# Seven half-width products in place of eight for the up projection of the last two token groups, with sums of weights made in the first group, and stores placed a step behind their data

## The chip, the cores and the metric

The kernel runs on one core of one Trainium2 chip. The metric is the device time of one execution in microseconds, the median of several runs. On the core, TensorE (PE in the profile, with its weight loads as PEld) multiplies, VectorE (DVE), ScalarE (ACT) and GpSimd (POOL) do the elementwise work, and SyncE (SP) issues every DMA of this kernel, from one queue that is worked off in order.

## What is computed

One inference step of a decoder layer with two kinds of mixer, for a prompt of 2048 tokens and 8 single-token samples (2056 columns in all). The model width is 1024, the feed-forward width 4096.

```python
h = rmsnorm(x, ln_mix)
proj = h @ w_in                           # 1024 -> 3592
od = gated_delta(conv(proj[...]), ...)    # 4 heads x 128, chunked over the prompt
oa = dilated_attention(proj[...])         # 8 heads x 64, three (window, dilation) branches
x = x + concat([od, oa]) @ w_out          # 1024 -> 1024
h = rmsnorm(x, ln_ffn)
x = x + square(relu(h @ w_ffn_up)) @ w_ffn_down     # 1024 -> 4096 -> 1024
y = rmsnorm(x, ln_final)
```

The outputs are y for prompt and samples, the new convolution and delta states, and the keys and values (the samples' caches are copied through).

## The kernel before

Tokens lie on the free axis, features on the partitions. The 2056 columns are cut into four groups, `GROUPS`: three of 512 columns and a last one of 520, worked as two pieces of 260. Each group goes through the input projection (`in_proj`, 28 units of 128 output features), the output projection (`out_proj`, 8 units), the up projection (`up`, 32 units) and the down projection (`down`, 8 chunks c of 8 outputs m).

Every dense product is made in three passes at fp32 accuracy: a weight block arrives by DMA as `wraw` (128x1024, 512 KB), ACT rounds it to `whi`, POOL subtracts to get `wlo` in four pieces of 256 columns (`load_w`), and PE adds up whi·hi, whi·lo and wlo·hi (`dense`, line 251) over eight 128-row blocks k, 24 matmuls for one unit and piece; `down` has 12, over four blocks. So POOL's part of a unit is needed for the last third of its matmuls. The split activations `hi`, `lo` stand in a pool of 32 tiles.

Two streams run beside each other. The dense stream goes through the phases in the order in_proj of groups 0 to 3, out_proj and the feed-forward part of groups 0 to 3. The mixer stream (`all_mixers`: delta rule, attention, then the samples, twice over the halves of the prompt) is a chain of Python generators; one step of it is taken after every 10 dense products of 512 columns (`advance`). Where a later phase needs the mixers' result, `drain` takes all steps that are left at once: `drain(1)` before `out_proj(0)`, `drain(3)` before `out_proj(2)`. Counted from the program, the mixers have 558 steps; `drain(1)` takes 15 of them, `drain(3)` takes 5. From group 2 on the dense stream is alone on PE.

`ffn` runs the up units four ahead of `down`: up 0 to 7, down(0), up 8 to 11, down(1), and so on; in chunk 7 the next group's `out_proj` stands ahead of down(7). `norm2` splits the next group's activations while `out_proj` runs. Work that ends later than its phase (`later`, one step after each dense unit) and the evacuations go to the lane "feed", and a scheduler orders the instructions of each engine from the lanes' priorities and its own estimate of when each is ready. Each DMA is issued where the code places it: a store such as `d_dn<-ct` in `evac_c` (line 406) follows its data at once, and everything behind it on SP waits until the data are there.

## Time and profile before

| what | value |
|---|---|
| median of 3 runs | 3067.29 us (3055.7 to 3068.8) |
| the profiled execution's own time | 3051.3 us, with a span of 3049.6 us |
| PE busy / DVE / ACT / POOL | 2922.2 / 1682.6 / 1248.5 / 1380.4 us |
| granted TensorE clock, mean | 0.981 |

The profiled execution is 16 us under the median, so sums are made against 3051.3 us and then carried over to the median. Stretches of time in the profile are given in us from the span's start. By the first evacuations of each phase (lines 1477, 1534 and 1555), out_proj(0) starts near 999, up of group 0 near 1062, down near 1113, out_proj(1) near 1540, out_proj(2) near 2175, the up of group 2 near 2251, out_proj(3) near 2590, and the up of group 3 near 2677. A busy PE is not PE at its peak, since the ends of matmuls are modelled; how fast it streams is read from the distance between evacuations.

### The profile page before, as it was taken

To read this page: it belongs to the slowest core of one execution; us is meant where nothing else is said; L and a number is where in the kernel's file an instruction comes from. 1 tells how busy PE (TensorE), PEld (TensorE's weight loads), DVE (VectorE), ACT (ScalarE), POOL (GpSimd) and SP (SyncE) were. 2 spreads that over 40 slices of the span, in tenths; PEclk is the share of its full clock that TensorE was granted. 3 is DMA by queue.
4 is the path that set the end of the run, shared out by engine and by line. 5 is a ranking of instruction groups with operands and counts; after the bars stand their busy time and mean duration, and the time that the engine had idled before them with its cause. 6 is when DMAs were issued, how large, how long until landed. Compare 5 with 4: busy or idle time off the path is not lost.

```text
span 3049.6 us, 49363 instructions
## 1 busy us (share of the span) xinstructions
PE 2922.2 (96%) x17793; PEld 2453.3 (80%) x17793; DVE 1682.6 (55%) x4200; ACT 1248.5 (41%) x2624; POOL 1380.4 (45%) x1743
## 2 busy tenths in 40 slices
PE   8999998999997999999999999999899999999997
PEld 6778776778896877777877778877788888999997
DVE  7657577665566744444467757467543223443334
ACT  5334335555552444544533433222342333433333
POOL 5546453323331343333344543455455555554554
PEclk9999999999999999999999999999999999999999
DMA  4566866665556555345368467477535444332322
GB/s 154 167 211 219 250 217 162 182 177 143 146 148 196 173 164 147 103 136 140 100 221 252 150 212 214 151 230 248 177 128 190 135 138 162 110 117 92 96 90 77
DMA packets 346643, 497.51 MB, mean 163 GB/s; under 512 B 74776, under 2 KB 245240, under 8 KB 341280
## 3 DMA queue, kind: packets, MB, share of 16 engines
q1 hardware_dynamic: 346400, 494.36, 53.4%
q8 instruction: 141, 2.31, 0.3%
q14 instruction: 102, 0.84, 0.1%
HBM read 413.56 MB, written 147.88 MB: 184 GB/s over the span
## 4 chain that ended last, share of the span: by engine, by line
PE 61%; DVE 4%; DMA 4%; issue 1%; POOL 1%; ACT 1%; SPq 1%; DVEq 0%; POOLq 0%; ACTq 0%
PE dense L251 49%; PE bank L936 2%; PE bank L892 2%; PE bank L949 1%; PE bank L910 1%; POOL wlo L232 1%; DMA dx<-d_dn 1%; PE bank L706 1%; PE bank L708 0%; PE bank L733 0%; PE bank L723 0%; PE bank L742 0%; PE bank L920 0%; DMA dw<-d_gc 0%; DMA dti<-d_t 0%
## 5 line engine op out<-in xcount | busy, mean ns | idle before, releaser
L232 POOL TENSOR_TENSOR wlo<-wraw,whi 128x256 fp32r<-128x256 f32 x1616 | 1269.2, 817 | 1454.0 <-ACT whi L229 868.6
L251 PE MATMUL dense<-s,whi 128*128 128x512 f32 (+2 forms) x8000 | 1689.9, 356 | 27.1 <-ACT whi L229 13.6
L251 PEld LDWEIGHTS dense<-s,whi 128*128 128x128 f32 x8000 | 1301.8, 190 | 237.9 <-issue 19.5
L251 PE MATMUL dense<-s,wlo 128*128 128x512 f32 (+2 forms) x4000 | 887.3, 354 | 0.0
L251 PEld LDWEIGHTS dense<-s,wlo 128*128 128x128 f32 x4000 | 659.6, 190 | 103.8 <-issue 3.7
L229 ACT ACTIVATE whi<-wraw 128x1024 fp32r<-128x1024 f32 x404 | 426.9, 1057 | 699.2 <-PE dense L251 588.3
L1555 DVE TENSOR_TENSOR y<-dense,y 128x512 f32<-128x512 f32 (+1 forms) x320 | 186.4, 583 | 306.1 <-PE dense L251 305.8
L880 ACT ACTIVATE as<-as,as 128x256 f32<-128x256 f32 (+2 forms) x384 | 169.7, 443 | 155.2 <-DVE as L876 153.0
L1534 DVE SCALAR_TENSOR_TENSOR tmp<-dense,rb 128x512 f32<-128x512 f32 (+1 forms) x160 | 93.4, 583 | 231.5 <-PE dense L251 231.0
L876 DVE CUSTOM_DVE_ANT_0 as<-bank,nd 128x256 f32<-128x256 f32 (+2 forms) x384 | 122.1, 350 | 171.3 <-PE bank L936 118.4
L1538 DVE TENSOR_TENSOR s<-tmp,s 128x512 fp32r<-128x512 f32 (+1 forms) x160 | 115.2, 720 | 132.7 <-ACT s L1537 132.6
L1536 ACT ACTIVATE tmp<-tmp 128x512 f32<-128x512 f32 (+1 forms) x160 | 87.6, 548 | 237.0 <-DVE tmp L1534 236.9
L403 DVE SCALAR_TENSOR_TENSOR cy<-cr,cw,cy 128x512 f32<-128x512 f32 (+3 forms) x189 | 148.0, 784 | 29.3 <-ACT cy L401 25.8
L892 PE MATMUL bank<-ident,as 128*128 128x128 f32 (+1 forms) x600 | 110.7, 288 | 3.4 <-ACT as L880 3.1
L892 PEld LDWEIGHTS bank<-ident,as 128*128 128x128 f32 (+1 forms) x600 | 64.1, 137 | 33.2 <-issue 17.4
L936 PE MATMUL bank<-ak,aql 128*128 128x256 f32 x256 | 89.3, 360 | 1.2 <-DVE aql L221 1.1
L1537 ACT ACTIVATE s<-tmp 128x512 fp32r<-128x512 f32 (+1 forms) x160 | 87.4, 547 | 4.5
L936 PE MATMUL bank<-ak,aqh 128*128 128x256 f32 x256 | 88.2, 356 | 0.0
L910 PE MATMUL bank<-ak,aq 128*64 128x64 f32 (+1 forms) x512 | 71.0, 375 | 13.6 <-issue 12.0
L949 PE MATMUL bank<-apt,av 128*64 128x128 f32 x944 | 82.0, 286 | 0.0
L382 ACT ACTIVATE ct<-cy 128x512 f32<-128x512 f32 (+3 forms) x83 | 44.0, 532 | 85.9 <-DVE cy L403 56.1
L383 DVE SCALAR_TENSOR_TENSOR ct<-ct,cy 128x512 f32<-128x512 f32 (+3 forms) x83 | 55.6, 670 | 39.6 <-ACT ct L382 38.8
(345 smaller groups left out, 2667.5 us busy)
## 6 DMA issues: line engine op xcount, KB each, us to landing
wraw<-wdn SPq DMA_DIRECT2D x132, 512.0 KB
wraw<-wup SPq DMA_DIRECT2D x128, 512.0 KB
wraw<-win SPq DMA_DIRECT2D x112, 512.0 KB
s_wk<-ck SPq DMA_DIRECT2D x64, 511.8 KB
s_wv<-cv SPq DMA_DIRECT2D x64, 511.8 KB
d_nak<-nak SPq DMA_DIRECT2D x16, 1024.0 KB
wraw<-wout SPq DMA_DIRECT2D x32, 512.0 KB
nak<-d_nak SPq DMA_DIRECT2D x16, 1024.0 KB
```

Source lines behind the costliest of these rows:

```text
L229: nc.scalar.activation(hi, raw, AF.Copy)
L232: nc.gpsimd.tensor_tensor(out=lo[:, c], in0=raw[:, c], in1=hi[:, c], op=OP.subtract)
L251: self.last = nc.tensor.matmul(p[:, :n], a[:, wo + k * 128:wo + (k + 1) * 128], x[k][:, off:off + n], start=first and i == 0 and k == ks[0 ...
L403: nc.vector.scalar_tensor_tensor(y[:, :np_], r[:, i:i + np_], self.cw[:, j, i:i + 1], y[:, :np_], op0=OP.mult, op1=OP.add)
L876: nc.vector.tensor_tensor_reduce(out=st[:, hh, :nk], in0=b["s"][hh], in1=b["nd"], op0=OP.add, op1=OP.min, scale=-(2.0 ** -(2 * j + hh + 1) ...
L880: nc.scalar.activation(st[:, hh, :nk], st[:, hh, :nk], AF.Exp, bias=so[:, i, hh:hh + 1], scale=-1.0, accum_out=so[:, i, 2 + hh:3 + hh])
L892: nc.tensor.transpose(pT[:m, w * 128:(w + 1) * 128], b["p"][:, hh, kb * 128:kb * 128 + m], self.ident)
L910: nc.tensor.matmul(p[64 * r:64 * r + 64, 256 * hh:256 * hh + nk], qr[hh][:, n:1024:16], ks[hh].bitcast(F32)[:, n:16 * nk:16], start=True, ...
L936: nc.tensor.matmul(p[:, 256 * hh:256 * hh + 256], x[:, q], ks[hh][:, k], start=n == 0, stop=n == 1)
L949: self.nc.tensor.matmul(po[s64, 128 * i:128 * i + 128], v[:, own - (nkb - 1 - kb) * step, s64], b["pt"][:, hh * nkb + kb, :], start=kb == ...
L1538: nc.vector.tensor_tensor(out=ul[:, s], in0=u[:, :n], in1=uh[:, s], op=OP.subtract)
L1555: self.last_v = nc.vector.tensor_tensor(out=y[m][:, s], in0=p[:, :n], in1=y[m][:, s], op=OP.add).ins
```

## The change

Two consecutive up units (2p and 2p+1) are taken as a 2x2 block matrix: rows are the two units, columns the two halves of k (k 0 to 3, k 4 to 7). The group's columns are cut into two halves too (256 each in group 2, 260 in group 3). In groups 2 and 3 the block product is made with seven products of 12 matmuls (Winograd's form of Strassen's scheme) where eight were.

- While group 0's up units go by, `sums_of_weights` makes four sums of each pair's blocks on POOL (4 adds of 128x512) and splits two of them (2 copies on ACT, 2 subtractions of 128x512 on POOL). Six stores of 256 KB for each of the 16 pairs go to `d_ws` (unsplit sums), `d_wh` and `d_wl` (split sums). The buffers of the split sums `wsh`, `wsl` have one copy each, the raw weights of group 0 and 1 four.
- In groups 2 and 3 `up_pair` loads four weight blocks for a pair: `wa` (unit 2p), `ws` (split sums, by two DMAs straight into whi and wlo), `wt` (unsplit sums), `wb` (half of unit 2p+1). POOL splits in pieces of 512 columns. Seven banks are read by one ACT copy and seven DVE adds.
- `norm2_sums` takes `norm2`'s place ahead of groups 2 and 3: for k 4 to 7 two scaled copies, four subtractions and seven splits of half width.
- After group 1 the weight pools are five deep for wraw, whi and wlo alike (before: wraw five, whi and wlo three); the space goes to the split sums of activations (`H2`).
- Stores: the evacuations of `in_proj` put their stores in a list that is issued one evacuation later (`store`, `flush`), with four buffers for `cy`, `ct`, `xs`. In the mixers a `yield` stands ahead of the stores of `dn_first`, `dn_turn` and `attn_combine`, and behind the loads of `attn_combine`; a `yield` after each of the first eight chunks of `delta_first` is taken out. Counted from the program the mixers now have 576 steps; `drain(1)` takes 18, `drain(3)` takes 20.
- `dynamic_dma_scratch_size=512` leaves more SBUF to the pools, and `late` adds two steps of slack in `rms_steps` after group 1.

```diff
+    def load_parts(self, hi, lo):
+        with self.lane("feed"):
+            w = self.wtile("whi", F32R), self.wtile("wlo", F32R)
+            for t, src in zip(w, (hi, lo)):
+                self.nc.sync.dma_start(t.bitcast(F32), src)
+        return w
...
     def evac_c(self, p, j, c0, n):
...
-        nc.sync.dma_start(self.d_dn[j, :, c0:c0 + np_], o[:, :np_])
+        self.store(self.d_dn[j, :, c0:c0 + np_], o[:, :np_])
...
+    def flush(self, keep):
+        while len(self.stores) > keep + 1:
+            for dst, src in self.stores.pop(0):
+                self.nc.sync.dma_start(dst, src)
...
     def dn_first(self, c):
...
+        yield 1
         nc.sync.dma_start(self.d_nak[c], nak)
...
     def delta_first(self, half):
...
                 yield from self.dn_first(c)
-                if c < 8:
-                    yield 1
...
+    def sums_of_weights(self, p, r1, r2):
...
+        s3 = total(a11, a21, OP.subtract)
+        s1 = total(a21, a22, OP.add)
+        s2 = total(s1, a11, OP.subtract)
+        s4 = total(a12, s2, OP.subtract)
+        yield 1
+        hl = parts(s1)
+        nc.sync.dma_start(self.d_ws[p, :, 0:512], s3)
+        nc.sync.dma_start(self.d_ws[p, :, 512:1024], s4)
+        yield 1
+        store(0, hl)
+        yield 1
+        hl = parts(s2)
+        yield 1
+        store(1, hl)
...
+    def norm2_sums(self, g, y):
...
+            sub(t1, a[:, m:n], a[:, 0:m])
+            sub(t2, b[:, m:n], t1)
+            sub(t3, b[:, m:n], a[:, m:n])
+            sub(t4, b[:, 0:m], t2)
+            for i, x in enumerate((a[:, 0:m], b[:, 0:m], b[:, m:n], t4, t1, t2, t3)):
+                s = self.H2.tile([128, GW], F32R, name="s2", tag="s2") if count < 16 else self.stile()
...
+                self.split(h, l, x, nc.vector)
...
+    def up_pair(self, g, p, h2):
...
+        wa = self.load_w(I["wup"][2 * p], 512)
+        ws = self.load_parts(self.d_wh[p], self.d_wl[p])
+        wt = self.load_w(self.d_ws[p], 512)
+        wb = self.load_w(I["wup"][2 * p + 1][:, 512:1024], 512)
...
+                for j, (a, x) in enumerate(((w[0], 0), (w[0], 1), (w[1], 0))):
+                    for k in range(4):
+                        c = 512 * half + 128 * k
+                        self.last = nc.tensor.matmul(bank[:, :m], a[:, c:c + 128], sets[i][k][x],
+                                                     start=j == 0 and k == 0, stop=j == 2 and k == 3).ins
...
+        q = product(wa, 0, 0)
+        with self.lane("feed"):
+            nc.scalar.activation(c11, q, AF.Copy)
+        q = product(ws, 1, 5)
+        add(c22, q, c11)
+        add(c11, product(wa, 1, 1), c11)
+        self.next_later()
+        add(c12, product(ws, 0, 4), c22)
+        q = product(wt, 0, 6)
+        add(c21, q, c22)
+        add(c22, q, c12)
+        add(c12, product(wt, 1, 2), c12)
+        square(u[0])
+        add(c21, product(wb, 0, 3), c21)
+        square(u[1])
```

Three places show how instructions moved. The first is POOL's row at the start of group 0's up units. `wlo` is the split of a weight block, `dw<-dS` the decay of the delta state in the mixers, `wsum` and `wsl` the sums and their split. Before:

```order
L716 TENSOR_TENSOR dw<-dS,egl 128x512 x4
L232 TENSOR_TENSOR wlo<-wraw,whi 128x256 x12
L716 TENSOR_TENSOR dw<-dS,egl 128x512
L232 TENSOR_TENSOR wlo<-wraw,whi 128x256 x8
L716 TENSOR_TENSOR dw<-dS,egl 128x512
L232 TENSOR_TENSOR wlo<-wraw,whi 128x256 x12
```

And now:

```order
L757 TENSOR_TENSOR dw<-dS,egl 128x512 x4
L257 TENSOR_TENSOR wlo<-wraw,whi 128x256 x12
L1553 TENSOR_TENSOR wsum<-wraw 128x512 x2
L757 TENSOR_TENSOR dw<-dS,egl 128x512
L1553 TENSOR_TENSOR wsum<-wsum,wraw 128x512
L231 TENSOR_TENSOR wsl<-wsum,wsh 128x512
L257 TENSOR_TENSOR wlo<-wraw,whi 128x256 x4
L1553 TENSOR_TENSOR wsum<-wraw,wsum 128x512
L231 TENSOR_TENSOR wsl<-wsum,wsh 128x512
L257 TENSOR_TENSOR wlo<-wraw,whi 128x256 x4
```

Between two units' splits there now stand the six POOL instructions of a pair, and the delta state's decay stands among them.

The second is PE's row at the end of the mixers, ahead of `out_proj(2)`. `bank<-ones,savc` sums the values of one sample (four matmuls, eight samples), rows of 8 and 4 matmuls are `down`, rows of 16 and 8 are units of `out_proj`. Before:

```order
L1384 MATMUL bank<-ones,savc 128x1 x4
L251 MATMUL dense<-s,whi 128x512 x4
L251 MATMUL dense<-s,wlo 128x512 x4
L251 MATMUL dense<-s,whi 128x512 x8
L251 MATMUL dense<-s,wlo 128x512 x4
L1384 MATMUL bank<-ones,savc 128x1 x4
L1389 MATMUL bank<-ident,apr 128x8 x4
L1384 MATMUL bank<-ones,savc 128x1 x4
L251 MATMUL dense<-s,whi 128x512 x16
L251 MATMUL dense<-s,wlo 128x512 x8
```

And now:

```order
L276 MATMUL dense<-s,wlo 128x512 x4
L1427 MATMUL bank<-ones,savc 128x1 x4
L276 MATMUL dense<-s,wlo 128x512 x4
L276 MATMUL dense<-s,whi 128x512 x9
L1427 MATMUL bank<-ones,savc 128x1 x4
L276 MATMUL dense<-s,whi 128x512 x7
L276 MATMUL dense<-s,wlo 128x512 x8
L1427 MATMUL bank<-ones,savc 128x1 x4
L276 MATMUL dense<-s,whi 128x512 x16
L1427 MATMUL bank<-ones,savc 128x1 x4
L276 MATMUL dense<-s,wlo 128x512 x8
L1427 MATMUL bank<-ones,savc 128x1 x8
```

The last six samples now stand among the first three units of `out_proj(2)`, where before only the last two stood behind the last `down`.

The third is SP's row in group 2's up units. Before, one load for each unit (`s_wk`, `s_wv` are pieces of the cache copy):

```order
L227 DMA wraw<-wup 128x1024 x2
L1590 DMA s_wk<-ck 368x356
L227 DMA wraw<-wup 128x1024 x2
L1590 DMA s_wv<-cv 368x356
L227 DMA wraw<-wup 128x1024 x3
```

And now:

```order
L244 DMA whi<-d_wh 128x1024
L244 DMA wlo<-d_wl 128x1024
L252 DMA wraw<-wup 128x1024
L252 DMA wraw<-d_ws 128x1024
L1786 DMA s_wk<-ck 368x356
L252 DMA wraw<-wup 128x512
L244 DMA whi<-d_wh 128x1024
L244 DMA wlo<-d_wl 128x1024
```

The two direct loads of a pair's `ws` stand behind the raw loads of the pair after it, and they have to wait until PE lets go of the whi and wlo tile that is five back.

More of the change, by code (lines that the diff above doesn't have):

```diff
@@ L326, in in_proj @@
                     with self.lane("feed"):
+                        self.flush(1)
                         getattr(self, "evac_" + kind)(p, i, c0, n)
+                        self.stores.append([])
+        with self.lane("feed"):
+            self.flush(0)
         if g == 3:
@@ L1441, in load_mix, with load_m @@
                 yield 1
+    def load_m(self, g, k):
+        g0, n = GROUPS[g][0][0], sum(n for _, n in GROUPS[g])
+        m = self.mtile(g) if g == 3 else self.P.tile([128, GW if g else 512], F32, name="m", tag="tmp" if g else "xs", bufs=None if g else 4)
+        self.nc.sync.dma_start(m[:, :n], self.d_mix[k, :, g0:g0 + n])
+        return m
     def mixed_tiles(self):
@@ L1567, in ffn @@
             uu, h2 = {}, self.next_up
[L1568 to L1569 removed]
+            self.ups(g, 0, h2, uu)
             for c in range(8):
[L1571 to L1572 removed]
+                if c < 7:
+                    self.ups(g, 4 * c + 4, h2, uu)
+                if c == 6 and g == 2:
+                    with self.lane("feed"):
+                        self.coming_m = [self.load_m(3, k) for k in range(2)]
                 if c == 7 and g < 3:
@@ L1603, in program @@
         b = Build(nc, tc, ctx, I, O)
-        b.W, b.ahead = ctx.enter_context(b.pool("W", 3)), 3
+        W = ctx.enter_context(b.pool("W", 3))
+        b.pools = {n: [W] * 3 for n in ("wraw", "whi", "wlo")}
         b.H = ctx.enter_context(b.pool("H", 32))
@@ L1623, in program @@
         Ys.insert(0, ctx.enter_context(b.pool("Y3", 8)))
+        sums = ExitStack()
+        b.SW = sums.enter_context(b.pool("S", 1))
+        b.pools["wraw"] = [W] * 3 + [b.SW]
         def late():
-            b.W, b.ahead = ctx.enter_context(b.pool("W3", 3, side="right")), 5
+            sums.close()
+            W3 = ctx.enter_context(b.pool("W3", 1, side="right"))
+            b.pools = {"wraw": [W] * 3 + [W3] * 2, "whi": [W] * 3 + [W3] * 2, "wlo": [W] * 3 + [W3] * 2}
+            b.turns = {}
+            b.late = True
+            b.H2 = ctx.enter_context(b.pool("H2", 16, side="right"))
             b.out = ctx.enter_context(b.pool("out", 1, side="right"))
```

158 lines of the change are left out of this document (127 added, 31 removed).

## The prediction

> **What bounds the kernel now.** I read the page first, then the busy times by stretch, then the waits, and last the instructions in order of time at the few places where PE stands idle.
>
> ```profile
> span 3049.6 us, 49363 instructions
> PE 2922.2 (96%) x17793; PEld 2453.3 (80%) x17793; DVE 1682.6 (55%) x4200; ACT 1248.5 (41%) x2624; POOL 1380.4 (45%) x1743
> PEclk9999999999999999999999999999999999999999
> ```
>
> PE is busy for 96% of the span at a clock that hardly dips, so only two things can move the time: PE's own work, and the 127 us in which it idles. The stretches tell where those are (columns: PE, PEld, DVE, ACT, POOL busy us with counts, granted clock, DMA share, GB/s).
>
> ```profile
> 450.00:470.00 20.00, 7.10 (x34) 5.23 (x33) 18.79 (x36) 5.62 (x11) 11.30 (x12) 0.78 0.78 193
> 900.00:1000.00 100.00, 81.05 (x723) 71.83 (x724) 61.01 (x202) 30.41 (x95) 23.52 (x30) 0.90 0.63 190
> 1062.00:1113.00 51.00, 49.88 (x235) 39.72 (x234) 26.21 (x53) 22.02 (x35) 27.32 (x38) 1.00 0.63 171
> 1113.00:1540.00 427.00, 425.24 (x2598) 327.14 (x2596) 197.89 (x671) 215.06 (x565) 137.63 (x174) 1.00 0.45 125
> 1540.00:1700.00 160.00, 145.15 (x720) 118.63 (x720) 113.24 (x284) 56.19 (x82) 78.11 (x101) 0.98 0.75 235
> 2100.00:2200.00 100.00, 85.86 (x390) 69.58 (x389) 56.95 (x88) 26.79 (x35) 45.52 (x53) 0.93 0.53 174
> 2251.00:2590.00 339.00, 339.00 (x1480) 274.71 (x1480) 109.13 (x157) 115.62 (x145) 195.80 (x246) 1.00 0.48 154
> 2677.00:3000.00 323.00, 323.00 (x2697) 323.00 (x2697) 106.72 (x232) 109.35 (x175) 165.42 (x224) 1.00 0.32 99
> ```
>
> The feed-forward parts of groups 2 and 3 (the last two rows) have no idle time on PE at all: work taken off PE there is time, as long as nothing else fills the gap. In group 0 (the third and fourth row) PE idles 3 us in 478, but there POOL gets new work. The idle time stands at four places: before the first attention (450 to 470, 12.9 us), in the drain before out_proj(0) (900 to 1000, 19.0 us), in the second half's delta rule (1540 to 1700, 14.9 us), and in the drain before out_proj(2) (2100 to 2200, 14.1 us).
>
> **PE's work in groups 2 and 3.** What a matmul costs is read from distances: evacuations at line 1555 stand 12 matmuls apart, and at the very start the kernel has matmuls of 256 columns in a row.
>
> ```profile
> 2400.19 0.69 DVE L1555 TENSOR_TENSOR y<-dense,y 128x512 f32<-128x512 f32 x1 [2.09 <-PE dense L251]
> 2402.97 0.69 DVE L1555 TENSOR_TENSOR y<-dense,y 128x512 f32<-128x512 f32 x1 [2.09 <-PE dense L251]
> 2802.39 0.43 DVE L1555 TENSOR_TENSOR y<-dense,y 128x260 f32<-128x260 f32 x1 [1.01 <-PE dense L251]
> 2803.83 0.43 DVE L1555 TENSOR_TENSOR y<-dense,y 128x260 f32<-128x260 f32 x1 [1.00 <-PE dense L251]
> 19.82 1.11 PE L251 MATMUL dense<-s,wlo 128*128 128x256 f32 x8
> 20.77 2.06 PE L251 MATMUL dense<-s,whi 128*128 128x256 f32 x16
> 22.67 1.11 PE L251 MATMUL dense<-s,wlo 128*128 128x256 f32 x8
> ```
>
> 512 columns: 2.78 / 12 = 0.2317 us. 260 columns: 1.44 / 12 = 0.1200 us. 256 columns: 24 matmuls from 19.82 to 22.67, 2.85 / 24 = 0.1188 us. Group 2 now has 16 pairs x 7 products x 12 = 1344 matmuls of 256 columns for 32 x 24 = 768 of 512: 159.7 for 177.9 us, a gain of 18.2, not the eighth (22.2) that the count of products promises, since halves cost 2.5% more than a whole. Group 3 was in halves already: 1344 for 1536, 192 x 0.1200 = 23.0 us less. Together **-41.2**. The bounds are tight: if 256 columns took as long as 260, -39.6; at half of 512, -45.
>
> Rule against row: the Trainium skill, "TensorE: Matmul & The Clock Gate", section "Back-to-back issue gap", gives for a stream of weight loads and matmuls a sustained 131 ns at 512 columns and 81 ns at 128, the spacing being set by both operations. On a straight line between them 256 columns would take some 98 ns, an estimate from that page, and group 2's change would be 1344 x 0.098 - 768 x 0.131 = +31 us. This trace disagrees: 0.2317 and 0.1188.
>
> **What feeds PE there.** POOL, DVE and ACT are 58%, 32% and 34% busy in group 2, and a pair adds one half block to POOL's four (+25% on up), and small adds on DVE that read seven banks in turn; they are hidden, and I cost them at nothing. The direct loads of `ws` are not hidden so surely. A pair lasts 84 x 0.1188 = 10.0 us; where two pairs follow each other without a `down` between them, the tile for the second pair's `ws` is let go after the first pair's third product (4.3 us) and needed at the second product of the next (11.4 us): 7.1 us for two blocks of 512 KB, behind raw loads on SP. The nearest rows are one such block alone, and the highest rate seen:
>
> ```profile
> 2175.43 4.06 DMA wraw<-wout
> 2190.00:2200.00 10.00, 10.00 (x45) 8.09 (x44) 4.46 (x5) 3.87 (x5) 5.82 (x8) 1.00 0.99 299
> ```
>
> At 299 GB/s two blocks (1.05 MB) need 3.5 us plus the latency; one after the other 8.1 us, 1.0 us late. There are 9 such places in each group (pairs 1, 2, 3, 5, ... 15), so 0 to +18; side by side is nearer, as both are issued together, and I take **+3**. The traffic grows by 2.6 MB for each chunk of 42 us (62 GB/s on 154), below the 299. `norm2_sums` puts 11 DVE instructions of half width for each of four k behind out_proj's last units: 44 x 0.54 (the row below) = 24 us, under units 5 to 7 and down(7), 16.7 + 22.2 us of PE: hidden, bound 0 to +6.
>
> ```profile
> L1538 DVE TENSOR_TENSOR s<-tmp,s 128x260 fp32r<-128x260 f32 x5 | 2.7, 535 | 2.3 <-ACT s L1537 2.3
> ```
>
> **The sums in group 0.** Sixteen pairs x six POOL instructions of 128x512. Of that size POOL has a row of its own:
>
> ```profile
> L1144 POOL TENSOR_TENSOR ao<-ao,ao 128x512 f32<-128x512 f32 x14 | 18.5, 1320 | 25.8 <-DVE ao L1142 25.2
> L232 POOL TENSOR_TENSOR wlo<-wraw,whi 128x256 fp32r<-128x256 f32 x32 | 25.4, 823 | 25.4 <-ACT whi L229 16.7 <-ACT dw L749 8.3 <-issue 0.4
> ```
>
> 96 x 1.32 = 127 us of POOL. After 1113 it fits: twelve pairs need 95 us, with 137.6 makes 233 of 427. In the eight units from 1062 to 1113 it does not: 27.3 + 24 x 1.32 = 59 us in a stretch of 51, so POOL is the bound there by **+8**. The delta state's decay, which stands among the sums in POOL's row, comes late by up to a pair's 7.9 us; PE's delta steps wait for that in part: **+4**. Behind a late `wsl` the stores wait on SP, and raw weights behind those; ACT's second `wsh` of a pair waits for the store of the first. Where splits run 10 us ahead of PE this is covered. Bounds for all of group 0: 0 (all in POOL's gaps) to +30 (each of the 16 pairs 1.9 us late).
>
> Two-input work on POOL also slows DVE. In the trace line 403's instruction takes 0.74 us and, once POOL runs its splits, 1.21:
>
> ```profile
> 463.06 0.74 DVE L403 SCALAR_TENSOR_TENSOR cy<-cr,cw,cy 128x512 f32<-128x512 f32 x1
> 463.90 3.88 POOL L232 TENSOR_TENSOR wlo<-wraw,whi 128x256 fp32r<-128x256 f32 x4 [1.89 <-ACT whi L229]
> 464.02 1.21 DVE L403 SCALAR_TENSOR_TENSOR cy<-cr,cw,cy 128x512 f32<-128x512 f32 x1
> ```
>
> With DVE at 46% busy from 1113 to 1540, I cost that at nothing; were all its 198 us to overlap with POOL's 127 new ones, it would still have a third of the stretch free.
>
> **The stores and the steps.** Before the first attention PE waits 10.4 us for queries and 2.5 for DVE; the loads of the queries (line 977) stand on SP behind stores of line 406 that wait for DVE.
>
> ```profile
> PE bank L910 <- issue: 10.4, 1, 10.4
> PE dense L251 <- DVE cr L389: 2.5, 1, 2.5
> 461.45 0.33 SPq L406 DMA_DIRECT2D d_dn<-ct  x1
> 462.43 1.09 SPq L977 DMA_DIRECT2D aq<-d_q  x2
> 468.67 0.33 SPq L406 DMA_DIRECT2D d_dn<-ct  x1
> 471.02 0.45 SPq L977 DMA_DIRECT2D aq<-d_q  x1
> ```
>
> The changed order keeps these rows' places, but each store now carries the data of the evacuation before, which are there. The loads then go out some 7 us sooner; DVE is 94% busy in this stretch and becomes the next bound. Between 0 and -12.9 I take **-8**. In the second half's delta rule the waits of line 613 (POOL's `nak`) move off SP, and eight more steps spread its loads; of 14.9 us idle I take **-3** (0 to -10).
>
> ```profile
> SPq L613 <- POOL nak L600: 35.1, 9, 6.7
> ```
>
> The eighteen added steps have a price. Drain(1) takes 18 for 15; at 19.0 us of idle time for 15 steps, three more cost **+4** (0 to +10). Drain(3) takes 20 for 5: five more samples of the value loop fall behind the last dense product that pays for steps. In the trace its end looks like this:
>
> ```profile
> 2169.62 0.95 PE L1384 MATMUL bank<-ones,savc 128*128 128x1 f32 x8
> 2173.70 1.05 PE L1384 MATMUL bank<-ones,savc 128*128 128x1 f32 x8 [2.79 <-DVE savc L1378]
> 2180.68 1.65 PE L251 MATMUL dense<-s,whi 128*128 128x512 f32 x3 [5.93 <-ACT whi L229]
> L1373 DVE TENSOR_TENSOR skt<-skt,apT 128x512 f32<-128x512 f32 x16 | 12.5, 815 | 0.0
> L1378 DVE TENSOR_TENSOR savc<-savc,skt 128x512 f32<-128x512 f32 x16 | 11.5, 717 | 0.2
> ```
>
> PE waits for DVE, and then 5.9 us for a weight that was queued behind the samples' last store. A sample is 3 x 0.815 + 2 x 0.717 = 3.9 us of DVE, five more 19.4. The changed PE row puts three units of out_proj (3 x 24 x 0.2317 = 16.7 us) among them, but DVE must also split that projection's inputs and evacuate it, some 8 us; the fourth unit's weight still waits for the end. 19.4 + 8 - 16.7 = 11, less what the first units' earlier weights save: **+7** (0 to +19).
>
> **Sum.** -41.2 + 3 + 8 + 4 - 8 - 3 + 4 + 7 = -26.2. On the profiled execution that is 3025, on the median of 3067.3, 16 us above it, **3041**. I predict for the median.
>
> **Rivals.**
> A, no change: group 0 gives the gain back. Each of 16 pairs is 1.9 us late (+30 for my +12), and nothing comes from the stores (+11): -26.2 + 18 + 11 = +3, 3070. For it: three engines and SP now wait on each other through buffers with one copy. Against: POOL's gaps after 1113, 289 us for 95.
> B, slower: the direct loads set the pace in groups 2 and 3. SP issues them late, behind raw loads that wait for ACT and POOL. The change is slower by 15 us once the 18 tight places lose 44 together, 2.5 us each - that is, 9.6 us for the 7.1; at 4.06 us each, one block's time again, it is 18 x 4.06 - 3 = +70 on the sum: +44, 3111. Against: SP had no such backlog in group 2, and DMA is at half its share.
> C, the change doesn't do what it says: narrow matmuls are set by their weight loads, which double in number in group 2. For it: at 260 columns PEld is busy for all 323.0 us of the last stretch. Against: the 0.1188 at 256 columns has that already in it; group 2 gains nothing only from 0.2317 x 768 / 1344 = 0.1324 on. Then it is -26.2 + 18.2 = -8, 3059. The page's rule above stands on this rival's side.
>
> **Chances.** My forecast (a gain over 0.5%, 15 us, which is about what a measurement of this kernel tells from no change) 0.66, its own range 3003 to 3052: -41.2 - 12.9 - 10 = -64 at best. A 0.18, C 0.03, B 0.13. So faster 0.66, same 0.21, slower 0.13. The range takes in A whole and leaves B out: 3003 to 3070.
>
> **What would show it.** Evacuations of up in groups 2 and 3 1.42 us apart (1.44 in group 3) and no idle PE; up and down of group 2 through chunk 6 in 321 us for 339. In group 0, POOL near full from 1062 on and PE waiting for wlo, but not after the first `down`. The wait for queries near 460 gone. More idle time before out_proj(2). It is wrong if PE waits for whi or wlo at a pair's second product (B), or for wlo all through group 0 (A).

## The result and the profile after

The change makes the kernel slower: 3095.9 us (median of 4 runs, 3088.6 to 3105.1) against 3065.4 (4 runs, 3055.7 to 3068.8), a ratio of 1.0105 with a 95% interval of 1.0078 to 1.0133. The forecast was 3041, in a range of 3003 to 3070. The profiled execution of the changed kernel has a span of 3092.3 us, in the middle of its runs; the profiled one of before (3049.6) is one of the shortest of its own, so the traces stand 42.7 us apart where the medians stand 30.5.

The page of the changed kernel:

```profile
span 3092.3 us, 50899 instructions
PE 2908.9 (94%) x18177; PEld 2469.0 (80%) x18177; DVE 1857.4 (60%) x4432; ACT 1293.4 (42%) x2712; POOL 1547.6 (50%) x1743
PEclk9999999999998899999999999999999999999999
```

PE is busy for 13.4 us less than before, and idles 183 us for 127. The granted clock dips in two neighbouring slices of the page where it did not before. To see where, both spans are cut at the same events: the first evacuation of out_proj(0), the first of out_proj(1), the last of down(6) in group 1, the first of down in group 2, the first of down in group 3, and the end. Busy time by stretch, before (columns as in the prediction):

```profile
0.00:999.10 999.10, 937.22 (x5932) 780.85 (x5933) 659.23 (x1768) 463.03 (x1182) 412.12 (x512) 0.98 0.62 183
999.10:1642.30 643.20, 631.16 (x3802) 495.70 (x3801) 349.93 (x1060) 302.88 (x713) 240.94 (x309) 1.00 0.53 155
1642.30:2169.80 527.50, 500.95 (x2696) 407.66 (x2694) 351.22 (x769) 169.22 (x275) 250.51 (x306) 0.96 0.62 198
2169.80:2300.80 131.00, 122.28 (x542) 99.66 (x543) 63.77 (x97) 54.51 (x73) 78.37 (x94) 0.96 0.52 167
2300.80:2707.80 407.00, 405.50 (x2140) 345.76 (x2139) 139.26 (x228) 144.39 (x195) 226.65 (x290) 1.00 0.44 143
2707.80:3049.60 341.80, 325.13 (x2691) 323.65 (x2689) 119.23 (x281) 114.50 (x187) 171.78 (x234) 0.98 0.28 89
```

And the changed kernel, cut at the same events:

```profile
0.00:1000.90 1000.90, 938.55 (x5933) 785.56 (x5934) 661.63 (x1769) 462.09 (x1182) 410.29 (x512) 0.97 0.63 183
1000.90:1705.90 705.00, 645.40 (x3717) 504.44 (x3716) 352.88 (x991) 312.93 (x735) 360.97 (x402) 0.95 0.58 171
1705.90:2228.80 522.90, 501.44 (x2738) 408.54 (x2736) 360.58 (x812) 177.41 (x288) 252.88 (x319) 0.97 0.67 210
2228.80:2375.20 146.40, 128.33 (x725) 112.00 (x726) 110.03 (x186) 65.34 (x108) 79.56 (x74) 0.92 0.56 185
2375.20:2770.50 395.30, 389.64 (x2537) 354.65 (x2536) 217.43 (x359) 161.99 (x238) 250.51 (x244) 1.00 0.61 198
2770.50:3092.30 321.80, 305.51 (x2535) 303.85 (x2534) 154.82 (x319) 113.66 (x164) 193.41 (x195) 0.98 0.45 144
```

By rows the difference is +1.8, +61.8, -4.6, +15.4, -11.7 and -20.0, together +42.7. Most of the gain that was forecast for PE lies in the last two rows. The second row, group 0, where the sums are formed, takes all of it back and more: PE idles 59.6 us there for 12.0, though POOL is busy for only 361 of 705 us. The first row ends ahead of the sums, and in the other runs below with the same code up to there it is 994 to 1004 us long; so a few us more or less in it mean nothing.

What PE waits for most in that row (releaser, us in total, times, longest):

```profile
PE bank L932 <- ACT as L920: 10.3, 8, 2.8
PE bank L603 <- DMA dx<-d_dn: 8.1, 1, 8.1
PE bank L950 <- DMA ak<-d_kl: 8.1, 2, 5.7
PE bank L950 <- DMA aq<-d_q: 6.3, 1, 6.3
PE bank L706 <- DMA dt<-d_t: 5.8, 1, 5.8
```

It never waits there for `wlo` or `whi`: the dense products always have their weights. PE waits for attention and the delta rule, for exponentials (ACT) and for loads (SP). One such wait, in order of time, first SP's row and then PE's:

```profile
1246.81 0.45 SPq L1002 DMA_DIRECT2D ak<-d_kh  x1
1254.34 0.32 SPq L1572 DMA_DIRECT2D d_ws<-wsum  x1
1258.34 0.32 SPq L1573 DMA_DIRECT2D d_ws<-wsum  x1
1261.13 0.33 SPq L252 DMA_DIRECT2D wraw<-wdn  x1
1261.56 0.38 SPq L1563 DMA_DIRECT2D d_wh<-wsh  x1
1262.39 0.32 SPq L1563 DMA_DIRECT2D d_wl<-wsl  x1
1262.76 0.48 SPq L1003 DMA_DIRECT2D ak<-d_kl  x1
1269.14 1.16 PE L950 MATMUL bank<-ak,aq 128*64 128x128 f32 x8 [5.69 <-DMA ak<-d_kl]
```

The two halves of a key block are loaded 16 us apart, since four stores of sums stand between them in SP's row and each waits for its sum; PE then stands for 5.7 us. Over the whole of group 0's row, ACT and POOL wait for this on account of the sums:

```profile
ACT wsh L230 <- POOL wsum L1553: 58.2, 16, 7.2
ACT wsh L230 <- DMA d_wh<-wsh: 23.4, 8, 6.8
POOL wsum L1553 <- DMA wraw<-wup: 62.4, 15, 6.1
```

So there were at least four candidates: the stores in SP's row, ACT's `wsh` (behind which attention's exponentials wait), POOL's wait for a raw weight ahead of a sum, and POOL's 124 us of new work as such. PE has sixteen stalls of over 1 us in group 0, 55.5 us in all. I followed each back by hand through the rows: eleven (36.7 us) seem to end at a sum in POOL's row, four of them by way of SP, five by way of ACT, two in POOL's own row. That is a reading and not a measurement; the experiments had to say which of these mattered.

### The profile page after: what moved, and what is told of

Its sections match the earlier page's. It is cut to its first block, busy times and chain, and to the rows that moved or that the text cites. A ratio compares the mean times of both kernels' runs of the same rounds, so it can differ in the third digit from the quotient of the medians.

```text
span 3092.3 us, 50899 instructions
## 1 busy us (share of the span) xinstructions
PE 2908.9 (94%) x18177; PEld 2469.0 (80%) x18177; DVE 1857.4 (60%) x4432; ACT 1293.4 (42%) x2712; POOL 1547.6 (50%) x1743
## 5 line engine op out<-in xcount | busy, mean ns | idle before, releaser
L257 POOL TENSOR_TENSOR wlo<-wraw,whi 128x256 fp32r<-128x256 f32 (+1 forms) x1520 | 1312.5, 895 | 1250.6 <-ACT whi L254 683.0
L276 PE MATMUL dense<-s,whi 128*128 128x512 f32 (+2 forms) x6464 | 1437.8, 365 | 29.4 <-ACT whi L254 14.2
L276 PEld LDWEIGHTS dense<-s,whi 128*128 128x128 f32 x6464 | 1082.5, 192 | 219.0 <-issue 17.1
L254 ACT ACTIVATE whi<-wraw 128x1024 fp32r<-128x1024 f32 (+1 forms) x436 | 446.9, 1026 | 735.1 <-PE dense L276 506.8
L276 PE MATMUL dense<-s,wlo 128*128 128x512 f32 (+2 forms) x3232 | 749.3, 362 | 0.0
L276 PEld LDWEIGHTS dense<-s,wlo 128*128 128x128 f32 x3232 | 546.9, 190 | 93.4 <-issue 4.6
L443 DVE SCALAR_TENSOR_TENSOR cy<-cr,cw,cy 128x512 f32<-128x512 f32 (+3 forms) x189 | 145.7, 772 | 29.1 <-ACT cy L441 26.6
L1641 PE MATMUL bank<-s,whi 128*128 128x256 f32 (+1 forms) x1024 | 145.0, 284 | 0.0
L1641 PEld LDWEIGHTS bank<-s,whi 128*128 128x128 f32 x1024 | 133.0, 191 | 0.5
L1641 PE MATMUL dense<-s,whi 128*128 128x256 f32 (+1 forms) x768 | 108.2, 283 | 0.0
L1641 PEld LDWEIGHTS dense<-s,whi 128*128 128x128 f32 x768 | 99.0, 190 | 0.0
L950 PE MATMUL bank<-ak,aq 128*64 128x64 f32 (+1 forms) x512 | 70.0, 374 | 30.4 <-issue 13.4
L1647 DVE TENSOR_TENSOR tmp<-bank,tmp 128x256 f32<-128x256 f32 (+1 forms) x128 | 54.4, 425 | 52.5 <-PE bank L1641 50.7
```

Of the source, the lines that this page charges most:

```text
L254: nc.scalar.activation(hi[:, :n], raw[:, :n], AF.Copy)
L257: nc.gpsimd.tensor_tensor(out=lo[:, c], in0=raw[:, c], in1=hi[:, c], op=OP.subtract)
L276: self.last = nc.tensor.matmul(p[:, :n], a[:, wo + k * 128:wo + (k + 1) * 128], x[k][:, off:off + n], start=first and i == 0 and k == ks[0 ...
L443: nc.vector.scalar_tensor_tensor(y[:, :np_], r[:, i:i + np_], self.cw[:, j, i:i + 1], y[:, :np_], op0=OP.mult, op1=OP.add)
L950: nc.tensor.matmul(p[64 * r:64 * r + 64, 256 * hh:256 * hh + nk], qr[hh][:, n:1024:16], ks[hh].bitcast(F32)[:, n:16 * nk:16], start=True, ...
L1641: self.last = nc.tensor.matmul(bank[:, :m], a[:, c:c + 128], sets[i][k][x], start=j == 0 and k == 0, stop=j == 2 and k == 3).ins
```

## The experiments

Ratios are to the kernel before, run beside each kernel; its medians there were 3058 to 3065 us.

| kernel | median us | ratio, 95% interval |
|---|---|---|
| the change | 3095.9 | 1.0105, 1.0078 to 1.0133 |
| no sums | 3020.6 | 0.9867, 0.9849 to 0.9885 |
| sums, no stores of them | 3093.3 | 1.0100, 1.0073 to 1.0127 |
| stores of raw weights, no sums | 3037.3 | 0.9917, 0.9893 to 0.9941 |
| moved stores and steps only | 3051.1 | 0.9965, 0.9949 to 0.9982 |
| the same, paced | 3053.3 | 0.9971, 0.9959 to 0.9984 |
| wsh on POOL | 3091.1 | 1.0100, 1.0078 to 1.0123 |
| sums on DVE | 3058.2 | 0.9988, 0.9974 to 1.0003 |
| sums of a constant, no stores | 3082.6 | 1.0070, 1.0045 to 1.0094 |
| thin sums, no stores | 3026.4 | 0.9880, 0.9865 to 0.9895 |
| sums in group 1 | 3121.7 | 1.0186, 1.0170 to 1.0203 |
| sums split late | 3079.2 | 1.0059, 1.0037 to 1.0081 |
| split late, in group 1 | 3100.0 | 1.0118, 1.0103 to 1.0133 |
| the change, wide splits | 3093.6 | 1.0096, 1.0077 to 1.0115 |
| moved stores only, wide splits | 3056.3 | 0.9971, 0.9957 to 0.9984 |
| sums on DVE, wide splits | 3069.3 | 1.0017, 1.0002 to 1.0031 |
| split late, on DVE, wide splits | 3064.9 | 1.0009, 0.9996 to 1.0022 |
| sums spread | 3087.7 | 1.0090, 1.0055 to 1.0125 |
| sums on DVE, queued behind | 3077.0 | 1.0048, 1.0029 to 1.0066 |

Of the eighteen kernels after the first, nine have medians that lie outside every range that was set for them beforehand: those without sums and with stores of raw weights below; those with sums in group 1, with the moved stores and wide splits, both on DVE with wide splits, and the one on DVE queued behind above; the two that split late on POOL between two ranges.

### Are the sums the cost, and which part of them?

**No sums.** Groups 2 and 3 load other arrays of the same size.

```diff
-        ws = self.load_parts(self.d_wh[p], self.d_wl[p])
-        wt = self.load_w(self.d_ws[p], 512)
+        ws = self.load_parts(self.d_kh[p % 4, :, 0:1024], self.d_kl[p % 4, :, 0:1024])
+        wt = self.load_w(I["wup"][2 * p + 1], 512)
...
-            if g == 0 and f % 2:
-                self.later.append(self.sums_of_weights(f // 2, self.raw1, self.raw_up))
-                self.next_later()
```

> The changed kernel with the sums of the weights left out of group 0: no additions on POOL, no splits of sums, no stores of them. What groups 2 and 3 would load of them is loaded from other arrays of the same size (split keys of the attention for the two parts of ws, the raw second weight for wt), so the products there have the same shapes and other values. Theory S (the loss is made by the sums in group 0: there PE idles 59.5 us between the first evacuation of out_proj(0) and that of out_proj(1), for 11 before): about 48 us under the changed kernel, 3040 to 3058, so 0.3 to 0.8% faster than the kernel before. Rival M (the loss comes with the moved stores and the eighteen added steps, which shift the mixers' work against group 0's loads): 3080 or more.

The ratio is 0.9867: the sums cost 2.4% of 3065, some 73 us, more than the 48 that I read from the idle time. Group 0's row tells where the rest is (637.5 us, PE busy for 624.4 at a clock of 0.99):

```profile
1001.90:1639.40 637.50, 624.37 (x3738) 491.62 (x3737) 340.33 (x1013) 297.42 (x706) 238.98 (x306) 0.99 0.53 152
```

The same matmuls took PE 645.4 us in the changed kernel, at a clock of 0.95: of the 67.5 us between the two rows 47 are idle time and 21 are slower matmuls.

**Sums without their stores; stores without sums.** The first keeps all arithmetic and drops the six stores of a pair; the second stores six halves of raw weights at the same places and forms no sums. The diff is that of the first; its groups 2 and 3 load other arrays, as in the kernel without sums.

```diff
-                nc.sync.dma_start(d[p, :, 512 * i:512 * i + 512], t.bitcast(F32))
+                pass
...
-        nc.sync.dma_start(self.d_ws[p, :, 0:512], s3)
-        nc.sync.dma_start(self.d_ws[p, :, 512:1024], s4)
```

> The changed kernel with the sums computed and split on POOL and ACT as they are, but the six stores of each pair left out; groups 2 and 3 load other arrays of the same size as in the kernel without sums. Theory S1 (the stores are the cost: they wait in SP's row for POOL and ACT, 133 us in all, and the loads of attention and delta rule stand behind them): nearly all of the loss goes, 3045 to 3062. Rival S2 (the arithmetic is the cost: POOL's additions ahead of its splits, and ACT's wsh, which waits 92 us for POOL and for stores with attention's exponentials behind it): 3080 to 3096.

> The changed kernel with no arithmetic for the sums, but with the six stores of each pair at their places, each of the same 256 KB taken from the raw weights, so that groups 2 and 3 load values other than the sums. The stores then wait for nothing but the weight's own load. Rival S3 (the cost of the stores is their traffic, 25 MB, and their 96 issues on SP): 3075 to 3096. Theory S1 (the cost is that they wait for POOL and ACT in SP's row): 3045 to 3062; raw weights are held a step or two longer for the stores, which is the reason for more than the 3048 of the kernel without sums.

My first theory (S1, the stores in SP's row) fell. Without any store of a sum the kernel is as slow, 1.0100. Its row for group 0 is even longer, though the profiled execution is the slowest of its four:

```profile
1004.50:1719.70 715.20, 647.04 (x3745) 505.01 (x3744) 351.35 (x1013) 313.48 (x738) 362.84 (x404) 0.95 0.47 135
```

The stores alone, which wait only for a weight's load, take 0.9917 - 0.9867 = 0.5%, 15 us: their traffic, their issues and the longer hold on the raw weights. The waits that the SP rows above show are real, but with them gone PE waits as long for something else. The row also bounds what POOL does to DVE: the same 1013 DVE instructions take 351.4 us for 340.3, so 11 us of DVE's own time in this row.

**Moved stores and steps only.** The rest of the change is undone (eight products everywhere, no sums, the pools as before).

> The kernel before with only the second half of the change: stores of in_proj a step behind their data, the added steps, the deeper buffers that go with them; eight products in all groups, no sums. The prediction's terms for this half cancel (-8 and -3 of idle time, +4 and +7 for the drains): 3060 to 3070 for 3065. Theory D (the drain ahead of out_proj(2) with 20 steps for 5 is the dear part, and the stores bring nothing, since the first out_proj began 1.8 us later in the changed kernel): 3070 to 3085. If the stores do what they were meant to and the drains are hidden: 3045 to 3057.

0.9965, 11 us faster than before: better than the prediction's zero, and the fastest of the kernels that do the whole computation. The two profiled executions don't show this gain (spans of 3050.1 and 3049.6 us), since that of before is a short one; what follows is idle time by row. In the second half's stretch the row is 515.1 us for 527.5 before, with 16.7 us of idle time for 26.6; ahead of group 2 it is 147.7 for 131.0:

```profile
1638.90:2154.00 515.10, 498.37 (x2718) 406.60 (x2717) 351.15 (x792) 173.30 (x282) 244.74 (x309) 0.97 0.63 206
2154.00:2301.70 147.70, 132.15 (x582) 109.22 (x582) 80.86 (x122) 54.52 (x73) 77.95 (x94) 0.91 0.48 160
```

**The same, paced**, so that drain(3) has 6 steps and not 20.

```diff
-STEPS = 10, 10
+STEPS = 10, 9.6
```

> The kernel with only the moved stores and steps (3051), with a mixer step for each 9.6 dense products in the second half in place of 10, so that 6 steps are left for the drain ahead of out_proj(2), not 20. Theory D (the twenty steps cost 17 us: from the last evacuation of down(6) of group 1 to the first down of group 2 it took 147.7 us for 131.0 before): 3033 to 3044. The prediction's +7 for this drain: 3042 to 3048. Rival (the steps cost the same wherever they stand): 3047 to 3056.

0.9971, no gain. The steps cost the same wherever they stand: the last stretch came back to 132.6 us, and group 0 became 17.5 us longer.

### ACT, the wait for raw weights, or POOL's time?

**wsh on POOL; sums of a constant; sums on DVE.**

```diff
-            self.split(h, l, t, nc.gpsimd)
+            nc.gpsimd.tensor_copy(h, t)
+            nc.gpsimd.tensor_tensor(out=l, in0=t, in1=h, op=OP.subtract)
```

> The whole change, but the upper part of a sum (wsh) is copied by POOL, not by ACT. Theory A (ACT is the cost: in the kernel without the stores it stands idle for 100 us in 32 places ahead of wsh, waiting for POOL, with attention's exponentials and the weights' upper parts behind it in its row): 3050 to 3075 for 3096. Rival V (the volume on POOL is the cost: 96 instructions of 1.29 us, now 32 copies more): 3096 to 3120. Rival W (POOL stands idle 62 us in 15 places ahead of a sum for a raw weight that has not landed, with splits and decays behind): no better than 3085.

1.0100: ACT's 82 us of waiting are gone, the loss is not. As POOL got 32 copies more, this alone doesn't clear ACT.

```diff
-        a11, a12, a21, a22 = r1[:, 0:512], r1[:, 512:1024], r2[:, 0:512], r2[:, 512:1024]
+        a11 = a12 = a21 = a22 = self.still
...
-            t = S.tile([128, 512], F32, name="wsum", bufs=4)
+            t = S.tile([128, 512], F32, name="wsum", bufs=3)
```

The constant takes the place of one buffer of the sums.

> The kernel without the six stores (3093), with the additions reading one constant tile in place of the raw weights; the volume on POOL and ACT's splits are the same, but no sum waits for a load, and no raw weight is held for a sum. Theory W (sums wait for weights): 3030 to 3055. Theories A and V (ACT waits for POOL; POOL's volume): 3075 to 3095.

1.0070, but not the test that I meant it to be: with nothing to wait for, all 96 instructions were scheduled in one burst ahead of out_proj(0). The two stretches, up to the first evacuation of out_proj(0) and on to that of out_proj(1):

```profile
941.00:1065.80 124.80, 64.48 (x451) 53.75 (x449) 92.42 (x147) 35.18 (x88) 116.50 (x99) 0.59 0.32 99
1065.80:1707.80 642.00, 624.87 (x3739) 491.48 (x3738) 341.10 (x1013) 299.34 (x709) 241.89 (x309) 0.99 0.53 152
```

Group 0 is as clean as without sums (642.0 for 637.5), and the drain before it takes 124.8 us with POOL full. In the kernel without sums it takes 60.9 from the same point:

```profile
941.00:1001.90 60.90, 46.18 (x422) 40.63 (x420) 39.50 (x144) 17.63 (x59) 4.16 (x4) 0.78 0.61 194
```

The loss went where POOL's work went, but its way here is another than in group 0. DVE takes 92.4 us for nearly the same instructions (147) for which it takes 39.5 (144) with POOL nearly idle, 53 us more in a drain that got 64 longer. As far as these rows tell, it is DVE that passes the sums' time on here, so this run says little on group 0; the last section has the instructions that got slower.

```diff
-            nc.gpsimd.tensor_tensor(out=t, in0=a, in1=b, op=op)
+            nc.vector.tensor_tensor(out=t, in0=a, in1=b, op=op)
...
-            self.split(h, l, t, nc.gpsimd)
+            self.split(h, l, t, nc.vector)
```

> The whole change, but the six operations of each pair run on DVE in place of POOL: 96 of some 0.67 us, 64 us on an engine that is busy for 340 of 637 us in group 0. If the loss comes of a slow engine that others wait for (theories A and V alike): 3045 to 3075, since the kernel without sums took 3020.6 and the stores' traffic 17 of what it lost. If it comes of the wait for raw weights wherever the sum stands (theory W), or if DVE, which stands in attention's own chain, is no better a place: 3080 to 3110.

0.9988: on DVE, where an addition takes 0.73 us for POOL's 1.29, the sums cost about half as much, although DVE stands in attention's own chain.

**Thin sums** tell the sums' length from their waits for raw weights: the same 96 and 32 instructions, on 16 columns, no stores.

```diff
-            nc.gpsimd.tensor_tensor(out=t, in0=a, in1=b, op=op)
+            nc.gpsimd.tensor_tensor(out=t[:, 0:16], in0=a[:, 0:16], in1=b[:, 0:16], op=op)
...
-            self.split(h, l, t, nc.gpsimd)
+            self.split(h[:, 0:16], l[:, 0:16], t[:, 0:16], nc.gpsimd)
```

> The kernel without the six stores (3093), with the same 96 instructions on POOL and 32 on ACT, each on 16 columns in place of 512: the same waits for raw weights and of ACT for POOL, but nearly none of POOL's 124 us; groups 2 and 3 load other arrays, and the sums are not complete. Theory V (the loss is POOL's time, which makes the splits, the decays and what waits for them late): 3022 to 3045. Theory W (it is the waiting, of POOL for raw weights and of ACT for POOL, and the longer hold on raw weights): 3070 to 3093.

0.9880, against 1.0100 with full columns: 2.2%, 67 us, hangs on the length of the sums' instructions, and 0.1%, within the noise, on their waits for raw weights, their holds on them and their number. POOL still waits 60.3 us for raw weights ahead of the sums (62.4 in the changed kernel); with short sums behind them these waits cost next to nothing. The row for group 0:

```profile
1003.40:1646.30 642.90, 626.05 (x3739) 492.75 (x3739) 339.14 (x1013) 301.98 (x738) 260.90 (x403) 0.99 0.52 151
```

**Fewer sums, another place.** Whole sums stored and split when loaded; sums formed in group 1; both.

```diff
-            if g == 0 and f % 2:
+            if g == 1 and f % 2:
                 self.later.append(self.sums_of_weights(f // 2, self.raw1, self.raw_up))
```

> The whole change, but s1 and s2 are stored as they are (two stores more of raw sums in place of four of parts), and groups 2 and 3 split them when they load them, as they do s3 and s4. Group 0 is rid of 32 of POOL's 96 instructions and of all of ACT's 32; POOL in group 2 gets 2.6 us more for each pair of 10.0, beside 58% busy time. Theory V (in proportion to POOL's time, 83 us for 124, and 4 stores for 6): 3055 to 3075. If ACT's waits are most of it: 3035 to 3055. If the split of ws sets the pace in group 2: over 3085.

> The whole change, but the sums are formed during group 1's up projection in place of group 0's. Attention is over by then; the delta rule's second half and the samples, with most of their work on DVE, run beside it. Theory P (the place is what makes it dear: attention's chain over PE, DVE, ACT and loads has no slack in group 0): 3035 to 3065. Theory V in its plain form (124 us on POOL cost some 58 wherever raw weights are split beside mixers): 3080 to 3100.

> Both together: whole sums stored, and formed in group 1. If the two gains add up: 3030 to 3055. If the place alone decides: as in the kernel with the sums in group 1.

With 83 us on POOL for 124 the ratio falls to 1.0059: group 0 takes 678.5 us, 41 over the kernel without sums, for 67.5 in the changed kernel, so about in proportion; 11 us are lost again around group 2, where `ws` now goes through ACT and POOL. Group 1 is no better but worse (1.0186, and 1.0118 with late splits): the place theory fell. The row with the sums in group 1, with the delta rule's second half and the samples, from the first evacuation of out_proj(1) to the last of down(6):

```profile
1633.00:2241.40 608.40, 521.67 (x2710) 419.10 (x2709) 380.21 (x783) 191.31 (x317) 381.33 (x413) 0.92 0.66 213
```

PE idles 86.7 us there, for 26.6 before.

### POOL's time as such, or the sums' own?

**Wide splits** take 35 us of other work out of POOL's row in group 0.

```diff
-        w = self.load_w(I["wup"][f])
+        w = self.load_w(I["wup"][f], 512)
...
-                w = self.load_w(I["wdn"][c, m // 2])
+                w = self.load_w(I["wdn"][c, m // 2], 512)
```

> The whole change, but the lower parts of up's and down's weights are split in two instructions of 512 columns (1.29 us each), not four of 256 (0.79): 35 us less on POOL in group 0, sums untouched. Theory V (POOL's time as such costs, some 0.5 us for each of its own): 3070 to 3083 for 3096. Rival B (only the sums' bursts and what waits for them cost): 3088 to 3100. A coarser split also lets a weight's first columns go half a microsecond later, which could cost in group 0's just-in-time loads.

> The kernel with only the moved stores and steps (3051), with the two wide splits in place of four for up's and down's weights. Where POOL is 38% busy in group 0 and no sums stand in its row, its time should cost nothing: 3045 to 3055 under rival B. Under theory V taken linearly (35 us in group 0 and as much in each later group, at 0.5) it would win 20 or more: under 3035.

> The whole change with the sums on DVE (3058), with the wide splits. Under rival B, as POOL has no sums any more: 3050 to 3062. Under theory V: 3035 to 3048.

> The whole change with only four sums of a pair formed, on DVE (47 us of it for 92 with the parts), stored whole in four stores and split when groups 2 and 3 load them, with wide splits. From the runs so far: 3020.6 without sums, + 11 for four of six stores (17), + 11 for half of what DVE's sums cost (21), + 10 for the first pairs of groups 2 and 3, where POOL stood behind (9 us of idle for 4 in each, in the kernel with late splits): 3040 to 3060. If the wide splits help as theory V says: 3030 to 3040.

None gained: 1.0096 for the change's 1.0105, 0.9971 for 0.9965 with the moved stores only, and on DVE 1.0017 for 0.9988, worse. The fourth, where I had added up what the single runs promised, took 3064.9 us and lies over its range: their gains don't add up. POOL's busy time in group 0 fell by 22 us (339.4 for 361.0), not by 35, so theory V's gain would have been some 12 us, 0.4%: at the edge of what the first pair's intervals can exclude, but the others went the wrong way. So nothing speaks for POOL's load as such as the cost; it is not excluded, since the coarser splits may themselves have cost something.

**Sums spread**: each operation queued behind the newest weight's split, additions in two steps of two.

```diff
-            nc.gpsimd.tensor_tensor(out=t, in0=a, in1=b, op=op)
+            with self.tc.issue_after(self.last_split):
+                nc.gpsimd.tensor_tensor(out=t, in0=a, in1=b, op=op)
...
         s1 = total(a21, a22, OP.add)
+        yield 1
         s2 = total(s1, a11, OP.subtract)
```

> The whole change, with every operation of the sums on POOL queued behind the newest weight's split (an order, not a wait), and the four additions taken in two steps of two: POOL never stands idle for a raw weight ahead of that weight's split, and no burst is over 2.6 us (5.2 before). POOL's time is the same. Theory B (the sums' place and bursts make the others late): 3050 to 3075. Rival R (their time costs wherever it stands in the row): 3085 to 3105; the raw weights are held about one weight longer, which could make it worse than 3096.

1.0090, 3087.7 us, in rival R's range. POOL no longer waits for a raw weight ahead of a sum, but SP now waits longer at the three lines of stores (219 us for the sums, 133 in the changed kernel):

```profile
SPq L1566 <- POOL wsl L231: 105.5, 31, 14.3
SPq L1577 <- POOL wsum L1555: 70.1, 16, 13.3
SPq L1576 <- POOL wsum L1555: 43.1, 16, 10.7
```

**Sums on DVE, queued behind** the newest evacuation in the same way.

> The whole change with the sums on DVE (3058), each operation queued on DVE behind the evacuation of the newest product at that point of the program (an order, not a wait), so that the raw weights have landed when DVE comes to the sums. Theory Q (what is left of the loss is DVE waiting 37.8 us for raw weights with attention's steps behind it): 3040 to 3052, which would beat the kernel with only the moved stores (3051) at best. Rival H (the wait is handed on to SP, whose stores then stand longer ahead of attention's loads, as in the spread sums): 3055 to 3070.

1.0048, worse than the sums on DVE as scheduled, and over the range of rival H too. SP's waits at the stores did grow, from 102 us to 142, as rival H has it. But the loss is not in group 0: that row is 662.5 us with 28.1 of idle time, for 673.8 with 37.5 in the sums on DVE as scheduled. It is in the row behind, up to the last of down(6) in group 1:

```profile
1658.60:2209.20 550.60, 508.36 (x2747) 414.79 (x2745) 361.94 (x837) 179.42 (x291) 251.38 (x320) 0.95 0.65 207
```

That row takes 521.6 us in the other kernel. PE waits in it 15.1 us for the delta rule's `dx` loads (1.8 in the other) and 9.9 for a reciprocal root, after the last store of a sum was issued. So in group 0 the order was a gain, as theory Q has it; why the next row loses 29 us stays open.

What this shows: the loss comes with the sums (no sums) and goes with the length of their instructions, 96 on POOL and 32 on ACT (thin sums); some of it stays wherever they were put, on POOL or DVE, in group 0, 1 or the drain. No single row is what passes it on to PE: taking away the stores, ACT's part, or POOL's waits for raw weights, each by itself, moved the ratio by 0.0015 at most, which is within the intervals. How the loss divides among these three when all stand together was not settled; no run took two of them away with the sums' length and place kept.

## Why the prediction was wrong, point by point

**The sums in group 0 (+8 and +4, bounds 0 to +30): the step that failed.** The row became 61.8 us longer. The instruction time was right (1.29 us for 1.32), and so was the sum (124 us for 127); wrong was to set it against POOL's gaps. I counted 233 busy us in 427 as room, and priced a late sum only where POOL would be full. Nor was POOL full there: from 1062 to 1113 POOL is busy for 28.6 us of 51, and PE never waits for `wlo`. POOL's row is in order, though, and so are SP's and ACT's, which take from it; PE's row has attention's and the delta rule's matmuls at fixed places, and nearly all its waits stand there. A burst of 5 us in a gap makes the next thing late in one of these rows, though the engine has time left on average; the rows of the stall at 1269 show one such case. On average each of the sixteen pairs came 3.9 us late, not 0.75 (12 / 16) and not the 1.9 of rival A. Rival A had the nearest reason ("three engines and SP now wait on each other") at half its size, and "POOL's gaps after 1113", the argument against it, was the error. But the sign that I gave for A, PE waiting for `wlo` all through group 0, did not come: the waits are attention's and the delta rule's. The step also left out what a stall does to the clock: of the 68 us by which group 0 is longer than without sums, 21 are slower matmuls.

**The rest of the sum holds, in part by luck.** Without the two terms for the sums it is -38; the kernel without sums came out at 0.9867, -41. But the stores and steps, which I had at 0 in all, gained 11 us by themselves, and the joints between the groups, which I had at 0 to +6, took some 10 of PE's 42: between the traces with the moved stores alone and without sums the spans differ by 32.3 us. Two misses of about 10 us cancel.

**PE's matmuls in groups 2 and 3 (-41.2): right.** From the first `down` of chunk 1 to that of chunk 5 in group 2, and of chunk 6 in group 3, before:

```profile
2344.20:2522.70 178.50, 178.50 (x770) 144.25 (x769) 44.87 (x65) 54.18 (x64) 97.71 (x129) 1.00 0.41 133
2753.90:2984.00 230.10, 230.10 (x1923) 230.10 (x1923) 71.38 (x161) 76.19 (x120) 116.65 (x161) 1.00 0.30 92
```

and after:

```profile
2416.90:2585.70 168.80, 168.80 (x1058) 151.74 (x1058) 78.80 (x122) 60.34 (x81) 108.51 (x105) 1.00 0.67 215
2812.70:3028.40 215.70, 215.70 (x1802) 215.70 (x1801) 101.99 (x191) 75.60 (x101) 135.88 (x131) 1.00 0.50 160
```

2.43 us less for each chunk of group 2 (2.28 forecast) and 2.88 in group 3 (2.88): 42 us over eight chunks each, with no idle time. Rival C is out. The Trainium skill, "TensorE: Matmul & The Clock Gate", section "Back-to-back issue gap", gives the sustained spacing that stood on its side; this trace disagrees with it, as group 2 gains 2.43 us a chunk where by that rule it would lose. The last two rows of the table of stretches keep 31.7 of the 42 us: the first four pairs of group 2 lie in the row before them, and the joints take the rest.

**The direct loads of `ws` (+3, up to +18) and rival B: nothing.** From group 2's up units on PE waits for them 0.2 us in all. **`norm2_sums` (0, up to +6): some +5 in PE's waits** for the reciprocal root at the joints ahead of groups 2 and 3, 6.9 us for 1.5 before; with the end of the kernel it is 9.8 in three places for 5.4:

```profile
PE fbank L223 <- DVE ry L182: 9.8, 3, 3.9
PE dense L1641 <- DMA wlo<-d_wl: 0.2, 1, 0.2
```

**The stores before the first attention (-8): nothing.** I took it that a store a step behind its data finds them there. From 452 to 472 us SP waited 11.8 us for `ct` before, and after:

```profile
SPq L384 <- DVE ct L423: 11.9, 2, 6.7
```

DVE itself is a step behind there (94% busy in the prediction's row), so the older data are as late as the newer were. **The second half (-3, to -10): about -10** of idle time with the stores alone, the bound; in the changed kernel -5 (21.5 us for 26.6). **Drain(1) (+4): can't be read.** out_proj(0) begins at 999.1 before and at 994 to 1004 in kernels with the same code up to there. **Drain(3) (+7): right in its idle time**, 15.6 us for 8.7 with the stores alone; but it is not worth avoiding, as the paced kernel shows.

## What to carry to other kernels

An engine that is half idle is no free place for work that others wait for in order: price new work by what stands behind it in each in-order row (here POOL's, ACT's, SP's and at last PE's), not by the sum of the gaps; and ask whether it makes another engine's instructions slower. When several rows pass a delay on, removing one of them shows nothing; shrink the work itself, as the thin sums did, to learn what it costs. Test the halves of a change apart: the half meant as a helper gained 11 us by itself, and the other half lost more than its 41 us of matmuls gained.

## What the hardware showed that was not expected

A stall of PE costs more than its own length. After the wait of 6.3 us at 1139 the first five matmuls of 512 columns take 2.08 us up to the next ones (1140.52 to 1142.60), 0.42 each, and the next eight 1.88 (to 1144.48), 0.235 each; the granted clock of the stall and of the stretch behind it is 0.69 and 0.74:

```profile
1139.44 1.16 PE L950 MATMUL bank<-ak,aq 128*64 128x128 f32 x8 [6.26 <-DMA aq<-d_q]
1140.52 2.24 PE L276 MATMUL dense<-s,wlo 128*128 128x512 f32 x5
1142.60 2.04 PE L276 MATMUL dense<-s,whi 128*128 128x512 f32 x8
1144.48 1.10 PE L276 MATMUL dense<-s,wlo 128*128 128x512 f32 x4
```

```profile
1133.00:1139.40 6.40, 0.17 (x1) 0.00 (x0) 1.27 (x1) 0.95 (x2) 1.89 (x3) 0.69 0.99 245
1139.40:1145.00 5.60, 5.56 (x24) 4.38 (x25) 0.83 (x2) 1.91 (x3) 3.37 (x4) 0.74 0.44 108
```

The Trainium skill, "TensorE: Matmul & The Clock Gate", section "What's actually happening", has half the clock after an idle window of some 3.4 us and full clock after a busy one. The trace agrees in both, with 0.42 us for 0.235 after 6.3 us of idle time, and the shorter time again some 3.2 us after PE went on. Over group 0, 47 us of idle time came with 21 us of slower matmuls, 68 of loss.

Beside POOL's additions of 128x512, one behind the other, small DVE instructions took five times as long. In the drain of the kernel without sums, and then in that of the sums of a constant, with all 96 POOL instructions of the sums (and ACT's 32 copies) in it:

```profile
L180 DVE SCALAR_TENSOR_TENSOR dt<-dt,dms 128x4 f32<-128x4 f32 x12 | 1.9, 156 | 0.2
L180 DVE SCALAR_TENSOR_TENSOR dt<-dt,dms 128x4 f32<-128x4 f32 x12 | 10.3, 859 | 0.2
```

DVE instructions of that drain that read a matmul's bank did not get slower (`dw<-bank,c` of 128x512: 692 and 682 ns). In group 0, where the sums stand apart, the same 1013 DVE instructions grew by 11 us in all.
